# A block of extra matmul runs, copies and transfers behind the last norm of a two-layer encoder trunk

## The chip, the cores and the metric

The kernel runs as one program on 1 core of one Trainium2 chip. The metric is device time in microseconds (us) of that core for one execution. A profiled execution has a span, from the first to the last instruction that the profile shows, and its own device time, which is a little longer.

## The reference

The reference is a hybrid bidirectional encoder of `DEPTH = 2` layers over one sequence of 512 positions with 1024 channels, all in float32:

```python
for l in range(DEPTH):
    xn = rms_norm(x, ln1[l])
    z = xn @ w_in[l]                       # one combined projection
    y_a = ...                              # gated linear recurrence, forward and backward
    y_b = spatial_gating(...)              # 128x128 position mixing
    y_c = window_attention(...)            # banded grouped-query attention
    merged = (gates[:, :, 0] * (y_a @ w_br[l, 0])
              + gates[:, :, 1] * (y_b @ w_br[l, 1])
              + gates[:, :, 2] * (y_c @ w_br[l, 2]))
    x = x + merged @ w_out[l]
    hn = rms_norm(x, ln2[l])
    x = x + jnp.square(jax.nn.relu(hn @ w_up[l])) @ w_down[l]
return rms_norm(x, final_norm)
```

Only the last line and the end of the second layer's MLP stand next to the change.

## The kernel before

All work is written in one function, `trunk`, over a tile framework: tiles come from pools by a tag with a fixed number of buffers (`T("rb", ...)`, `T("jk", ...)`, `PT("m", ...)` for PSUM), and a scheduler decides when each instruction is put into its engine's queue. It works by priority (by default the order of the program text) among the instructions whose inputs are ready in its own timeline, and it places the semaphores. `tc.issue_after(ins)` adds an edge of issue order behind `ins`; by the framework's code, only instructions of the same engine as `ins` get it. Each engine's queue is then executed in order.

Every large matmul is made from split operands: a float32 value is cast on ScalarE to the type fp32r (`wh`, `xh`, `sh`), the rest is taken by subtraction on VectorE (`wl`, `xl`), and three matmuls make one product. Their moving operand is read in "pairs" order: `pairs(t)` reads column 0, column 256, column 1, column 257 and so on, with 512 columns in all. Plain float32 matmuls (attention, transposes) read contiguously. Weights come in chunks `ws[i]` of 128 x 1024 float32 (512 KB) by DMAs from the SP queue into `wr` or `wq` tiles; the `wq` tag has 10 buffers.

The end of the program is the last quarter (`qd == 3`) of the second layer's MLP. `down` runs `seven`, a scheme of seven block products per half, and as results leave PSUM, `done` adds up the squares of a row block and `finish` scales it and sends it out:

```python
def finish(ts):
    ...
    nc.gpsimd.tensor_tensor(rc, ss, mhalf_t[:, 0:n], ALU.pow)
    for i, t in enumerate(ts):
        nc.scalar.activation(xr[t][0], xr[t][0], AF.Copy, scale=rc[:, i:i + 1])
        nc.vector.scalar_tensor_tensor(xr[t][1], xr[t][1], rc[:, i:i + 1], fn_t[1], ALU.mult, ALU.mult)
        for fl in range(2):
            q = nc.scalar if (t, fl) == (1, 0) else nc.sync
            q.dma_start(out[:, t, fl * S:(fl + 1) * S], xr[t][fl])
```

It is called for row blocks 2 and 3 together, then for block 0, and last for block 1. After it the pools are closed and the program ends. The tile `z4` (128 x 2048, one buffer) holds the final norm's weights `fn_t` at that point, and `wq` holds the last chunks of the down projection.

Of the kernel before, what the change touches and what calls it, by code (L numbers as in the profile page):

```python
# [6 lines left out]
F32 = mybir.dt.float32  # L7
F32R = mybir.dt.float32r
U8 = mybir.dt.uint8
AF = mybir.ActivationFunctionType  # L10
ALU = mybir.AluOpType

P = 128
S = 512
# [5 lines left out]
CW = 1024  # L20
# [9 lines left out]
def ap_of(t, off, dims):  # L30
    return bass.AP(tensor=t.tensor, offset=t.offset + off, ap=[t.ap[0]] + dims)
# [11 lines left out]
def natural(t):  # L43
    return t.rearrange("p (a b) -> p a b", a=2)


def sorted_(pt):

    return ap_of(pt, 0, [[1, 2], [2, S // 2]])


def _chunk_keys():
# [26 lines left out]
def trunk(tc, x0v, xT, xt, ws, fnb, bsb, snk, wst, rope, cmask, amask, ident, out):  # L79
    nc = tc.nc  # L80
# [3 lines left out]
    def pool(**kw):  # L84
        p = tc.tile_pool(**kw)
        pools.append(p)
        return p.__enter__()

    cst = pool(name="cst", bufs=1)
    sb = pool(name="sb", bufs=1)  # L90
# [3 lines left out]
    dram = pool(name="dram", bufs=1, space=bass.MemoryType.DRAM)  # L94
# [11 lines left out]
    part = {}  # L106
# [4 lines left out]
    def nm(s):  # L111
        ctr[0] += 1
        return f"{s}_{ctr[0]}"

    def T(tag, name, dt=F32):
        where = part[HOME[tag]] if tag in HOME else sb
        return where.tile([P, S], dt, tag=tag, bufs=SLOTS[tag], name=nm(name))

    def begin(which):
        part[which] = pool(name=nm(which), bufs=1)  # L120
# [8 lines left out]
    def Z4(name):  # L129
        z4[:] = [sb.tile([P, 4, S], F32, tag="z4", bufs=1, name=nm(name)), 0]  # L130
        return z4[0]
# [8 lines left out]
    def SM(tag, w):  # L140
        return pad.tile([P, w], F32, tag="sm_" + tag, bufs=4 if tag == "lb" else NSM, name=nm(tag))
# [7 lines left out]
    def PT(tag, name):  # L149
        return ps.tile([P, S], F32, tag="p_" + tag, bufs=BANKS[tag], name=nm(name))  # L150
# [101 lines left out]
    def proj_part(xs, pt, w, ks):  # L252

        hi, lo = w
        for k in ks:
            c = slice(k * P, (k + 1) * P)
            i = mm3(pt, hi[:, c], lo[:, c], xs[k][0], xs[k][1], k == 0, k == KT - 1)
        return i

    def proj(xs, name, *key, bank="m"):  # L260

        return proj_w(xs, name, wload(*key), bank=bank)
# [139 lines left out]
    def two(pr, i):  # L402
        return tuple(x[:, i * HT:(i + 1) * HT] for x in pr)
# [359 lines left out]
    for i in range(2):  # L763
        c = slice(i * S, (i + 1) * S)
# [20 lines left out]
    for i in range(8):  # L785
        t = T("tv", "xt")
# [11 lines left out]
    for l in range(DEPTH):  # L798
        xs = n1.xs

        def evac(pt, tag, name):
            t = T(tag, name)
            with hp():
                nc.vector.tensor_tensor(natural(t), sorted_(pt), natural(n1.rb), ALU.mult)
            return t

        def a_ffb(h):
            z2 = Z2("z2") if h else None
            parts = [z2[:, d] if h else T("zt", "z2") for d in range(2)]
            for d in range(2):  # L810
                pt = proj(xs, f'f{h}', l, 'f', h, d)
                with hp():
                    nc.vector.tensor_tensor(natural(parts[d]), sorted_(pt), natural(n1.rb), ALU.mult)
            return a_gates(l, h, z2 if h else parts, lbs)
# [48 lines left out]
        bv = [None] * 4  # L863
# [68 lines left out]
        if l == 0:  # L932
            amask_t = cst.tile([P, 7 * P], U8, name="amask_t")
            for i in range(2):
                w = slice(i * 448, (i + 1) * 448)
# [15 lines left out]
        run = a_head(l, 0, *head_0, vt, oa)  # L951
# [14 lines left out]
        for g in range(4):  # L966
            pt = PT("s", "mx")
# [20 lines left out]
        def merge_b(d):  # L988
            z = evac(proj(xs, "gz", l, "gz", d), "l2", "gz")
            with hp():  # L990
                nc.scalar.activation(z, z, AF.Tanh, scale=0.5)
            if d % 2 == 0:
                wbr[0] = wload(l, "yb", d // 2)
            yp = proj_w(ys, "yB", wbr[0], (d % 2) * 4)
            m = T("g", "mg")
            with hp():
                nc.vector.scalar_tensor_tensor(natural(m), natural(z), 1.0, sorted_(yp), ALU.add, ALU.mult)
            nc.gpsimd.dma_start(mgd[:, d], m)
# [46 lines left out]
        pt = PT("c", "vT")  # L1045
# [101 lines left out]
        with later(30000):  # L1147
# [5 lines left out]
            for fl in range(2):  # L1153
                th = gates("ch", 0, fl)
                pts = proj_tok(ys, "yC", (l, "y", 2, fl), 0)
                for t in range(4):
                    if fl == 0:
                        kept.append(T("l", "mC"))
                    m = th[t] if fl else kept[t]
# [51 lines left out]
        xr = [[T("l", "xr"), T("l", "xr")] for _ in range(4)]  # L1211
# [19 lines left out]
        i = proj_part(n2.xs, *first[0], range(4))  # L1231
# [18 lines left out]
        last = l + 1 == DEPTH  # L1250
        Z4("u")
        n1 = norm_tok("ln1", l + 1, xr, True, 1.0 / math.sqrt(D) if last else 1.0)
        acc = [[T("tv", "acc"), T("tv", "acc")] for _ in range(4)]
        fn_t = []

        def finish(ts):

            n = len(ts)
            ss = SM("s4", 4)[:, 0:n]
            nc.vector.scalar_tensor_tensor(ss, ap_of(n1.ss, 2 * ts[0], [[2, n]]), EPS, ap_of(n1.ss, 2 * ts[0] + 1, [[2, n]]), ALU.add, ALU.add)  # L1260
            rc = SM("rs", 4)[:, 0:n]
            nc.gpsimd.tensor_tensor(rc, ss, mhalf_t[:, 0:n], ALU.pow)
            for i, t in enumerate(ts):
                nc.scalar.activation(xr[t][0], xr[t][0], AF.Copy, scale=rc[:, i:i + 1])
                nc.vector.scalar_tensor_tensor(xr[t][1], xr[t][1], rc[:, i:i + 1], fn_t[1], ALU.mult, ALU.mult)
                for fl in range(2):
                    q = nc.scalar if (t, fl) == (1, 0) else nc.sync
                    q.dma_start(out[:, t, fl * S:(fl + 1) * S], xr[t][fl])

        def done(t, fl):  # L1270

            n1.add(t, fl)
            if not last:
                nc.gpsimd.dma_start(xspill[:, t, fl * S:(fl + 1) * S], xr[t][fl])
            if last:
                if fl == 0:
                    nc.vector.tensor_tensor(xr[t][0], xr[t][0], fn_t[0], ALU.mult)
                if (t, fl) in ((0, 1), (1, 1)):
                    finish((t,))
                elif (t, fl) == (3, 0):  # L1280
                    finish((2, 3))
            elif t % 2:
                n1.turn(fl, (t - 1, t), "ssaa" if (t, fl) == (1, 1) else "ssss")

        for qd in range(4):
# [11 lines left out]
            for f in range(8):  # L1297
                if qd == 0 and f < 3:
                    pt = first[f][0]
                    proj_part(n2.xs, *first[f], range(4, KT))  # L1300
                else:
                    pt = proj(n2.xs, f'up{qd}', l, "up", qd, f, bank="c" if qd == 0 and f == 3 else "m")
# [21 lines left out]
        if not last:  # L1324
# [4 lines left out]
            end("mlp")  # L1329
            begin("G")  # L1330
        xsrc = xspill

    for p in reversed(pools):
        p.__exit__(None, None, None)
# [124 lines left out]
```

## Time and profile before

| | before |
|---|---|
| median of 2 runs | 1632.4 us (1631.79 to 1633.01) |
| profiled execution, its own time | 1631.72 us |
| span of the profiled execution | 1629.6 us |
| instructions | 21891 |
| PE busy | 1606.6 us (99% of the span) |
| DVE busy | 1288.0 us (79%) |
| ACT busy | 990.8 us (61%) |
| POOL busy | 117.2 us (7%) |

The engines are PE (TensorE matmul), PEld (its weight loads), DVE (VectorE), ACT (ScalarE), POOL (GpSimd) and SP (SyncE, which here only issues DMAs). In a timeline row the first number is the start in us from the span's start, the second the time that the merged piece takes, then engine, line, operation, output<-input, shape and count; what an engine waited for stands in brackets. Matmuls are pipelined, so the rate of a run of matmuls is read from start to start, not from one matmul's duration.

### The profile page before, as it was taken

Reading aid. Unit: us, or ns where it says so; the run is one execution under the profiler, and the core shown is the slowest. Engines: PE = TensorE matmul, PEld = TensorE weight load, DVE = VectorE, ACT = ScalarE, POOL = GpSimd, SP = SyncE. Lnnn points to the kernel's source line nnn. Section 1 sums busy time; section 2 is a strip of 40 time slices with the busy share of each in tenths; the row PEclk is TensorE's granted clock in tenths of the full one; section 3 lists DMA queues with packets and bytes.
Section 4 is the critical chain, followed back from the end, with each engine's and each line's share of the span. In section 5 each row is a group of like instructions: output and inputs, shape, how many; then the busy total and the mean of one; then the engine's idle time right before and its main releaser. Section 6 shows DMA issues by size and latency. Waiting matters only on the chain.

```text
span 1629.6 us, 21891 instructions
## 1 busy us (share of the span) xinstructions
PE 1606.6 (99%) x8034; PEld 1411.1 (87%) x8034; DVE 1288.0 (79%) x2015; ACT 990.8 (61%) x1695; POOL 117.2 (7%) x169
## 2 busy tenths in 40 slices
PE   9999999999999999999999999999999999999997
PEld 8888888998888888888888888888898888888886
DVE  7996998785666768697989969987856677686967
ACT  7576678775245664545766667688753365545464
POOL 1021000011200000000010210000103000000000
PEclk9999999999999999999999999999999999999999
DMA  8342221232555323233423422212226453332321
GB/s 334 121 149 97 83 89 53 78 104 98 197 197 197 113 104 104 104 104 104 143 93 124 172 96 78 91 59 85 84 98 223 177 194 104 103 108 100 125 69 52
DMA packets 58138, 195.83 MB, mean 120 GB/s; under 512 B 7504, under 2 KB 7888, under 8 KB 58032
## 3 DMA queue, kind: packets, MB, share of 16 engines
q1 hardware_dynamic: 47520, 160.23, 28.2%
q0 software_dynamic: 10368, 33.96, 5.9%
q8 instruction: 63, 1.03, 0.3%
q14 instruction: 43, 0.35, 0.1%
q10 hardware_dynamic: 144, 0.26, 0.0%
HBM read 175.54 MB, written 18.87 MB: 119 GB/s over the span
## 4 chain that ended last, share of the span: by engine, by line
PE 72%; DVE 12%; issue 6%; ACT 6%; DMA 2%; POOL 1%; SPq 0%; POOLq 0%; DVEq 0%; ACTq 0%
PE up L250 7%; PE up L248 7%; PE up L249 7%; PE dA L467 3%; PE dA L468 3%; PE dA L466 3%; DVE wl L243 2%; DVE ex L667 2%; PE wo L299 2%; PE wo L300 2%; PE dC L467 2%; PE wo L301 2%; PE dC L466 2%; PE at L625 2%; PE dC L468 2%
## 5 line engine op out<-in xcount | busy, mean ns | idle before, releaser
L242 ACT CAST wh<-wq 128x1024 fp32r<-128x1024 f32 x201 | 210.3, 1047 | 169.5 <-PE dA L467 42.7
L243 DVE TENSOR_TENSOR wl<-wq,wh 128x1024 fp32r<-128x1024 f32 x201 | 244.1, 1219 | 85.6 <-ACT wh L242 84.6
L243 DVE TENSOR_TENSOR wl<-wr,wh 128x1024 fp32r<-128x1024 f32 x166 | 203.3, 1225 | 129.7 <-ACT wh L242 124.0
L242 ACT CAST wh<-wr 128x1024 fp32r<-128x1024 f32 x166 | 173.3, 1045 | 211.4 <-PE up L249 55.4
L248 PE MATMUL up<-xh,wh 128*128 128x512 f32 x512 | 194.2, 379 | 0.0
L249 PE MATMUL up<-xl,wh 128*128 128x512 f32 x512 | 194.0, 379 | 0.0
L250 PE MATMUL up<-xh,wl 128*128 128x512 f32 x512 | 193.1, 379 | 0.0
L250 PEld LDWEIGHTS up<-xh,wl 128*128 128x128 f32 x512 | 96.8, 189 | 13.7
L248 PEld LDWEIGHTS up<-xh,wh 128*128 128x128 f32 x512 | 96.8, 189 | 13.7
L249 PEld LDWEIGHTS up<-xl,wh 128*128 128x128 f32 x512 | 96.8, 189 | 13.7
L466 PE MATMUL dA<-wh,sh 128*128 128x512 f32 x256 | 97.1, 379 | 0.0
L467 PE MATMUL dA<-wh,sh 128*128 128x512 f32 x256 | 97.0, 379 | 0.0
L468 PE MATMUL dA<-wl,sh 128*128 128x512 f32 x256 | 90.3, 379 | 0.0
L667 DVE TENSOR_TENSOR ex<-ex 128x512 f32<-128x512 f32 x112 | 80.4, 735 | 3.1 <-ACT key L647 3.0
L625 PE MATMUL at<-qt,kt 128*128 128x128 f32 x448 | 64.1, 276 | 1.7 <-ACT yh L307 0.6
L639 ACT ACTIVATE qt<-ex 128x512 f32<-128x512 f32 x56 | 37.6, 671 | 42.4 <-DVE ex L667 25.5
L625 PEld LDWEIGHTS at<-qt,kt 128*128 128x128 f32 x448 | 58.3, 192 | 4.6 <-ACT on L726 0.9
L307 ACT CAST sh<-sf 128x512 fp32r<-128x512 f32 x64 | 39.6, 618 | 25.2 <-DVE sf L430 18.1
L468 PEld LDWEIGHTS dA<-wl,sh 128*128 128x128 f32 x256 | 48.4, 189 | 6.8
L466 PEld LDWEIGHTS dA<-wh,sh 128*128 128x128 f32 x256 | 48.4, 189 | 6.8
L467 PEld LDWEIGHTS dA<-wh,sh 128*128 128x128 f32 x256 | 48.4, 189 | 6.8
L1079 ACT ACTIVATE sc<-sc,mx 128x256 f32<-128x256 f32 (+1 forms) x64 | 35.3, 553 | 25.3 <-DVE mx L1077 25.3
(414 smaller groups left out, 4303.3 us busy)
## 6 DMA issues: line engine op xcount, KB each, us to landing
wr<-in_ws_dram SPq DMA_DIRECT2D x166, 512.0 KB, 3.3
wq<-in_ws_dram SPq DMA_DIRECT2D x117, 512.0 KB, 4.4
thd<-zt POOLq DMA_DIRECT2D x32, 256.0 KB, 2.5
th<-thd POOLq DMA_DIRECT2D x32, 256.0 KB, 3.2
mgd<-mg POOLq DMA_DIRECT2D x16, 256.0 KB, 2.4
mB<-mgd POOLq DMA_DIRECT2D x16, 256.0 KB, 5.8
xt<-in_xt_dram SPq DMA_DIRECT2D x8, 256.0 KB, 7.6
mcd<-th POOLq DMA_DIRECT2D x8, 256.0 KB, 3.2
```

What stands on the lines that cost most here:

```text
L242: cast_i[0] = nc.scalar.copy(hi, raw)
L243: nc.vector.tensor_tensor(lo, raw, hi.bitcast(F32), ALU.subtract)
L248: nc.tensor.matmul(o, whi, xh, start=first, stop=False)
L249: nc.tensor.matmul(o, whi, xl, start=False, stop=False)
L250: return nc.tensor.matmul(o, wlo, xh, start=False, stop=last)
L307: nc.scalar.copy(hi, src)
L466: nc.tensor.matmul(o, xh[:, t], h, start=start and k == 0, stop=False, skip_group_check=True)
L467: nc.tensor.matmul(o, xl[:, t], h, start=False, stop=False, skip_group_check=True)
L468: return nc.tensor.matmul(o, xh[:, t], l_, start=False, stop=k == 3, skip_group_check=True)
L625: nc.tensor.matmul(pt[:, c], kk(st), qq[:, c], start=True, stop=True)
L639: nc.scalar.activation(qt.rearrange(shp, b=nb, h=2), e_q, AF.Exp)
L667: nc.vector.tensor_tensor(o_ap, o_ap, ap_of(ex, i_, [[istep, 2]] + z), ALU.add)
```

## The change

A new function `bench` is called once, after both layers, with `last_out[0]`, the first half of the row block that `finish` scaled last. It computes nothing that the output reads. The recording line in `finish` is the only change to what was there.

```diff
+def bench(tc, nc, sb, dram, ws, PT, T, Z4, part, nm, last):
+    V = nc.vector
+    wh = sb.tile([P, CW], F32R, tag="wh", bufs=3, name=nm("bwh"))
+    wl = sb.tile([P, CW], F32R, tag="wl", bufs=3, name=nm("bwl"))
+    f32 = T("rb", "bf")
+    V.tensor_copy(f32, last)
+    for t in (wh, wl):
+        nc.scalar.copy(t[:, 0:S], f32)
+        nc.scalar.copy(t[:, S:], f32)
+    prev = [None]
+    sink = T("jk", "bs")
+
+    def run(n, rhs, cols, w):
+        pt = PT("m", "bm")
+        o = pt[:, 0:cols]
+        ...
+        for i in range(n):
+            c = slice((i % 4) * P, (i % 4 + 1) * P)
+            with tc.issue_after(prev[0].ins) if prev[0] is not None else contextlib.nullcontext():
+                prev[0] = nc.tensor.matmul(o, w[:, c], rhs, start=i == 0, stop=i == n - 1)
+        V.tensor_copy(sink[:, 0:cols], pt[:, 0:cols])
+        return pt
+
+    def two(t, n, gap):
+        return ap_of(t, 0, [[1, n // 2], [gap, 2]])
+
+    run(48, wh[:, 0:256], 256, wl)
+    run(48, two(wh, 256, 128), 256, wl)
+    run(48, two(wh, 256, 256), 256, wl)
+    run(48, two(wh, 128, 64), 128, wl)
+    run(24, wh[:, 0:384], 384, wl)
+    run(24, two(wh, 384, 192), 384, wl)
+    run(24, f32[:, 0:128], 128, f32)
+    run(24, two(f32, 128, 64), 128, f32)
+    run(12, f32[:, 0:256], 256, f32)
+    run(12, two(f32, 256, 128), 256, f32)
+    a = run(4, wh[:, 0:S], S, wl)
+    b = PT("c", "bs")
+    c = PT("c", "bt")
+    d = PT("a", "bv")
+    for _ in range(3):
+        nc.scalar.copy(b, a)                                              # A1
+        nc.scalar.copy(c, b)                                              # A2
+        nc.scalar.copy(d, f32)                                            # A3
+        nc.scalar.copy(f32, c)                                            # A4
+        nc.scalar.copy(natural(f32), sorted_(c))                          # A5
+        V.tensor_tensor(sink, sink, c, ALU.add)                           # V1
+        V.tensor_tensor(natural(sink), natural(sink), sorted_(c), ALU.add)# V2
+        V.tensor_tensor(c, f32, b, ALU.add)                               # V3
+        V.scalar_tensor_tensor(sink, c, 0.0, f32, ALU.max, ALU.mult)      # V4
+        V.scalar_tensor_tensor(sink[:, 0:256], f32[:, 0:256], 0.0, f32[:, 256:], ALU.max, ALU.mult)  # V5
+        V.tensor_copy(sink, d)                                            # V6
+    big = Z4("big").rearrange("p a b -> p (a b)")
+    q = [big[:, i * CW:(i + 1) * CW] for i in range(2)] + [part["wq"].tile([P, CW], F32, tag="wq", bufs=10, name=nm("bq")) for _ in range(6)]
+    with tc.issue_after(prev[0].ins):
+        nc.sync.dma_start(q[0], ws[0])
+        nc.sync.dma_start(q[1], ws[1])
+    for i in range(4):
+        with tc.issue_after(prev[0].ins):
+            nc.sync.dma_start(q[2 + i], ws[i])
+    for i in range(4):
+        nc.gpsimd.dma_start(q[2 + i], ws[i + 2], accum_op=ALU.add)
+    for i in range(4):
+        with tc.issue_after(prev[0].ins):
+            nc.sync.dma_start(q[6 + i % 2], ws[i + 20])
+    for _ in range(2):
+        V.tensor_tensor(big, big, big, ALU.add)
+        V.tensor_tensor(big.rearrange("p (a b) -> p a b", a=4)[:, :, 0:256], big.rearrange("p (a b) -> p a b", a=4)[:, :, 256:], big.rearrange("p (a b) -> p a b", a=4)[:, :, 0:256], ALU.subtract)
+        nc.scalar.copy(big, big)
...
+        last_out = [None]                          # beside fn_t, in the loop over layers
...
+                last_out[0] = xr[ts[-1]][0]        # in finish, behind the two scalings
...
+    bench(tc, nc, sb, dram, ws, PT, T, Z4, part, nm, last_out[0])   # behind both layers
```

The marks A1 to A5 and V1 to V6 are added here as names for the steps of the loop.

More of the change, by code (lines that the diff above doesn't have):

```diff
@@ L49, in sorted_ @@
     return ap_of(pt, 0, [[1, 2], [2, S // 2]])
+def bench(tc, nc, sb, dram, ws, PT, T, Z4, part, nm, last):
[12 more added lines that the diff above has]
+        o = pt[:, 0:cols]
+        if len(rhs.ap) == 3:
+            o = o.rearrange("p (a b) -> p a b", a=rhs.ap[1][1])
+        for i in range(n):
[49 more added lines that the diff above has]
+        nc.scalar.copy(big, big)
```

## The prediction

> **What bounds the kernel now.** I read the page's first parts, then the timeline of the last 10 us, because everything the change adds waits for the last norm.
>
> ```profile
> span 1629.6 us, 21891 instructions
> ...
> PE 1606.6 (99%) x8034; PEld 1411.1 (87%) x8034; DVE 1288.0 (79%) x2015; ACT 990.8 (61%) x1695; POOL 117.2 (7%) x169
> ```
>
> PE is busy for 99% of the span; the rest is the tail, which the timeline of the last microseconds shows:
>
> ```profile
> 1621.08 0.38 PE L468 MATMUL dA<-wl,sh 128*128 128x512 f32 x1
> ...
> 1624.27 0.55 POOL L1262 TENSOR_TENSOR rs<-s,mhalf_t 128x1 f32<-128x1 f32 x1 [1.70 <-DVE s L1260]
> 1624.86 0.72 ACT L1264 ACTIVATE xr<-xr,rs 128x512 f32<-128x512 f32 x1 [0.92 <-POOL rs L1262]
> 1624.86 0.75 DVE L1265 SCALAR_TENSOR_TENSOR xr<-xr,rs,u 128x512 f32<-128x512 f32 x1 [0.73 <-POOL rs L1262]
> 1625.61 0.40 ACTq L1268 DMA_DIRECT2D out_dram<-xr  x1
> ```
>
> The last matmul starts at 1621.08. The last `finish` is that of row block 1; its ScalarE half ends at 1624.86 + 0.72 = 1625.58, and this is the tile handed to `bench`. From there to 1629.6 only output transfers land and the engines close. So PE, DVE, ACT and POOL are all empty after 1625.6: whatever hangs on that tile is added behind it, with nothing of the old kernel to hide under.
>
> **The start of the new chain.** V copies the tile to `f32`, ACT casts it four times, the first matmul needs the first three (`wh` left, `wh` right ahead of it in order, `wl` left).
>
> ```profile
> L307 ACT CAST sh<-sf 128x512 fp32r<-128x512 f32 x64 | 39.6, 618 | 25.2 <-DVE sf L430 18.1 <-DVE sf L433 7.1
> L938 DVE CAST amask_t<-am 128x448 uint8<-128x448 f32 x2 | 0.7, 376 | 0.0
> L308 DVE TENSOR_TENSOR sh<-sf,sh 128x512 fp32r<-128x512 f32 x64 | 43.8, 685 | 1.5 <-ACT sh L307 0.4
> ```
>
> The DVE copy of 512 columns isn't in the trace. Below stands the 448-column one-input cast, 0.38; above, the two-input 0.69. I take 0.41, the cast scaled up. The ACT casts cost 0.62 each, so PE starts at 1625.6 + 0.4 + 3 x 0.62 + 0.1 for the hand-overs = 1628.0. If the framework waits for all four casts it is 0.6 more.
>
> **The matmul runs.** Prices are start-to-start distances. The first four rows are split matmuls in pairs order, attention's plain float32 and its 128-column form; then come contiguous fp32r scores at 384 and 256 columns.
>
> ```profile
> 1190.27 0.38 PE L248 MATMUL ag<-xh,wh 128*128 128x512 f32 x1
> ...
> 1191.57 0.38 PE L248 MATMUL ag<-xh,wh 128*128 128x512 f32 x1
> ...
> 1192.21 1.05 PE L625 MATMUL at<-qt,kt 128*128 128x128 f32 x8
> 1193.11 0.60 PE L1106 MATMUL po<-pT,cvt 128*128 128x256 f32 x2
> ```
> ```profile
> 256.14 0.34 PE L1072 MATMUL sc<-k,q 128*128 128x384 f32 x1
> 256.32 0.34 PE L1073 MATMUL sc<-kl,q 128*128 128x384 f32 x1
> 256.49 0.27 PE L1101 MATMUL pT<-id_t,sc 128*128 128x128 f32 x1
> ```
> ```profile
> 213.67 0.28 PE L1073 MATMUL sc<-kl,q 128*128 128x256 f32 x1
> ...
> 214.03 0.38 PE L248 MATMUL yB<-yh,wh 128*128 128x512 f32 x1
> ```
> ```profile
> 239.85 1.03 PE L1106 MATMUL po<-pT,cvt 128*128 128x256 f32 x4
> 240.72 0.49 PE L1101 MATMUL pT<-id_t,sc 128*128 128x128 f32 x3
> ```
> ```profile
> L1106 PE MATMUL po<-pT,cvt 128*128 128x256 f32 x160 | 40.0, 380 | 0.0
> ```
>
> - Pairs order, fp32r: six matmuls of 512 columns in 1191.57 - 1190.27 = 1.30, 0.217 each. Halved, 0.109 for 256 columns; three quarters, 0.163 for 384.
> - Contiguous fp32r: 256 columns, three in 0.36, 0.120 each; 384 columns, two in 0.35, 0.175. Contiguous is a little dearer than its share of a pairs matmul.
> - Plain float32: `po` is called 80 times in the two layers (10 blocks per head pair, 4 pairs) and has 160 records, so one call is two passes. A pass takes 0.2175 at 256 columns (four in 0.87) and 0.1125 at 128 (eight in 0.90).
>
> Runs 1 to 11 in the order of the program:
> 1. 48 x 0.120 = 5.8
> 2. and 3. 48 x 0.109 = 5.2 each, 10.4
> 4. 128-column fp32r in pairs: no row has it. Below: a quarter of 0.217, 0.054, makes 2.6. Above: what plain float32 pays for 128 columns, two passes, 0.225, makes 10.8. I take 0.1125, one pass with a weight load of its own, the nearest row in size: 5.4. The ends stay in the range, 2.8 below and 5.4 above.
> 5. 24 x 0.175 = 4.2
> 6. 24 x 0.163 = 3.9
> 7. and 8. 24 x 0.225 = 5.4 each, 10.8
> 9. and 10. 12 x 0.435 = 5.2 each, 10.4
> 11. 4 x 0.22 = 0.9
>
> Sum 51.8. Between runs PE stands still for nothing: two "m" banks alternate, and a copy of 0.7 on DVE is over long before the bank's next turn.
>
> One sentence on what a page says of run 4: in the Trainium skill, "TensorE: Matmul & The Clock Gate", section "LDWEIGHTS (loading the stationary operand)", a weight load takes its columns divided by 1.2 GHz, by which I estimate 0.107 a matmul and 5.1 for the run; no row here shows a weight load as the bound.
>
> **The clock.** PE has been still since 1621.5 when the runs start.
>
> ```profile
> 1624.70:1629.60 4.90, 0.00 (x0) 0.00 (x0) 0.75 (x1) 0.72 (x1) 0.12 (x1) 0.50 0.47 176
> ```
> ```profile
> 1.05 4.64 PE L186 MATMUL warm<-warm 128*128 128x512 f32 x10 [1.05 <-DVE warm L183]
> 5.48 1.66 PE L248 MATMUL bu<-xh,wh 128*128 128x512 f32 x4
> 6.98 1.03 PE L249 MATMUL bu<-xl,wh 128*128 128x512 f32 x4
> ```
>
> In the view by stretches (behind the busy times of the five engines stands the granted clock) the clock is 0.50 from 1624.7 on. The start of the program shows the price: 14 matmuls take 6.98 - 1.05 = 5.93, where at 0.217 they would take 3.04. I add this 2.9 to run 1; the bounds are 0 and twice that.
>
> A page gives another size: the Trainium skill, "TensorE: Matmul & The Clock Gate", section "Part 1: The HAM clock gate (the 'warmup' mystery)", has the full clock back after about 3.4 us of sustained work, which at half speed would cost an estimated 1.7. The sum would be 1.2 lower by it; the start here shows 2.9.
>
> PE thus ends at 1628.0 + 51.8 + 2.9 + 0.2 for the last matmul's tail = 1682.9.
>
> **The copy loop.** It waits for run 11 (`a`), the last in PE's order.
>
> ```profile
> L645 ACT COPY at<-at 128x512 f32<-128x512 f32 x8 | 4.6, 580 | 1.4 <-PE at L625 1.3
> L1307 ACT ACTIVATE u<-up 128x512 f32<-128x512 f32 x64 | 37.8, 591 | 0.0
> L429 DVE TENSOR_TENSOR sf<-u 128x256 f32<-128x256 f32 x32 | 13.6, 424 | 0.4 <-ACT u L1308 0.4
> L1019 DVE TENSOR_TENSOR cq<-cq,sh 128x512 f32<-128x512 f32 x8 | 5.8, 731 | 0.0
> L516 DVE SCALAR_TENSOR_TENSOR xr<-dA,r,xr 128x512 f32<-128x512 f32 x16 | 11.5, 741 | 0.1
> ```
>
> An ACT copy out of PSUM is 0.58; the strided `sorted_` read of L1307 costs no more (0.59). Copies into PSUM have no row; I take 0.6. On DVE V3 0.69, V4 0.74, V5 0.42; V6 lies between 0.41 and 0.69, I take 0.69 for a PSUM source: 2.54.
> Round 1: A1, A2, A4, A5 in a chain, 2.4 (A3 needs only `f32` and can go ahead during the runs); V1 and V2 (0.69 + 0.73) start behind A2 and end at 2.6. Then V3 to V6, each on the result or the tile of the one before, 2.54. Rounds 2 and 3: A1 needs V3 and A2 needs V4, both hidden beside V4 to V6, but A3 overwrites `d`, which V6 reads, and A4 overwrites `f32`, which A3 reads: 3 x 0.6 = 1.8, with V1 and V2 beside it, then 2.54. A hand-over takes 0.04 (L1262 ends at 1624.82, its readers start at 1624.86); with 0.4 for those of the loop: 2.6 + 3 x 2.54 + 2 x 1.8 + 0.4 = 14.2. Loop ends at 1697.1.
>
> **What I cost at nothing.** The two passes over `big` need only `q[0]` and `q[1]`.
>
> ```profile
> L606 ACT ACTIVATE ex<-ex 128x2048 f32<-128x2048 f32 x4 | 7.7, 1916 | 0.0
> L243 DVE TENSOR_TENSOR wl<-wq,wh 128x1024 fp32r<-128x1024 f32 x201 | 244.1, 1219 | 85.6 <-ACT wh L242 84.6
> wq<-in_ws_dram SPq DMA_DIRECT2D x117, 512.0 KB, 4.4
> mC<-mcd POOLq DMA_DIRECT2D x8, 256.0 KB, 9.4
> ```
>
> A pass is 2.3 (DVE, 2048 columns, twice the 1219 ns row less one overhead) + 1.2 + 1.9 = 5.4, two of them 10.8 plus hand-overs, 11. The loads overwrite `z4`, free at 1625.6, and land 4.4 later, about 1630; DVE and ACT are empty until 1683 but for short result copies, so the scheduler can place all of it under the runs. Without that cover it is 11 at the end.
> SP: the order edges name a PE instruction, and the framework applies them only to PE's, so the ten loads are not held; six can start as `wq` buffers fall free from about 1600 on, the two to `big` wait in SP's queue for 1625.6 with output transfers near them, which matter no longer.
> POOL: the four accumulating transfers have no row. Below stands the plain SP load of that size, 4.4, so 18 for four; above, the slowest POOL row (9.4 for 256 KB), doubled for size and one after the other, 75. From 1610 even that ends at 1685, before the loop does. So nothing.
>
> **The sum.** After the last work the engines close in about 1.0 (the outputs have long landed). Span 1698.1, that is 68.5 more; 1631.72 + 68.5 = 1700.2 in the profiled execution's terms; the median of the runs is 0.7 above it: **1701**.
>
> **Rivals.**
> - *`big` comes last*: the scheduler's order keeps the text's order on DVE. For it: the text puts it last. Against it: the scheduler works by what is ready, and DVE and ACT have nothing else for 50 us. 1701 + 11 = 1712.
> - *POOL holds something up*: an accumulating transfer queued ahead of L1262 makes the norm wait for its load, or four of them outlast the loop. The point is a load landing after 1619, or over 22 us a transfer. Price 5 to 40: 1706 to 1741.
> - *Pairs with small distances read slower*: the rows show distance 256 only. Doubled fp32r pairs runs (2, 3, 4, 6) are 19.7: 1721. The Trainium skill, "SBUF — State Buffer", section "Door 1: The DMA port swizzle", charges each access that leaves a 16-byte line; the pairs rows at 0.217 against 0.120 for half as many contiguous columns do not agree.
> - *Not slower*: nothing reads `bench`'s results; if the build drops unread work, place: all eleven runs, price -68: 1633. It decides once over 36 of the 68 is gone. Against it: the ten `warm` matmuls above, whose result is never read, ran.
> - *Everything at its low end* (run 4 at 2.6, no slow clock, short V6): 1694 and below.
>
> **How the numbers follow.** Forecast (1693 to 1709) 0.68; `big` last 0.10; POOL 0.10; pairs 0.04; dropped 0.03; low end below 1693 0.05. The range 1692 to 1716 holds the forecast, `big` last and half of POOL, over 0.8. Two per cent, about what a measurement of this kernel can tell, is 33 us: slower 0.97, within 0.03, faster 0.
>
> **What would show it.** PE's first new matmul near 1628 at clock 0.50 for some 5 us; runs at the distances above, run 4 anywhere from 0.054 to 0.225; the `big` instructions inside the runs' stretch; L1262 still near 1624; the loop about 14 us. Wrong would make it: distances over 0.13 at 256 columns, accumulations landing after 1695, copies into PSUM far from 0.6.

## The result and the profile after

The changed kernel takes 1706.87 us (median of 1705.36 and 1708.38) against 1632.4 before: a ratio of 1.0456, 95% interval 1.0411 to 1.0501. The profiled execution took 1705.36 with a span of 1703.4, so the span grew by 73.8. The forecast was 1701 with a growth of 68.5.

The first parts of the page of the changed kernel:

```profile
span 1703.4 us, 22771 instructions
...
PE 1662.2 (98%) x8422; PEld 1463.8 (86%) x8422; DVE 1312.4 (77%) x2049; ACT 1005.4 (59%) x1716; POOL 120.7 (7%) x173
```

PE has 388 matmul records and 55.6 us more. The rest of the 73.8 lies where PE does nothing: ahead of run 1 and behind run 11.

The timeline of VectorE in the changed kernel; L1339 is the last norm's scaling, L58 the copy to `f32`, L74 the copy of a run's result, which starts some 0.2 us behind the run's last matmul (the first two are held up by the work on `big`):

```profile
1623.98 0.75 DVE L1339 SCALAR_TENSOR_TENSOR xr<-xr,rs,u 128x512 f32<-128x512 f32 x1 [0.73 <-POOL rs L1336]
1624.73 0.43 DVE L58 COPY bf<-xr 128x512 f32<-128x512 f32 x1
1632.24 2.29 DVE L120 TENSOR_TENSOR big<-big 128x2048 f32<-128x2048 f32 x1 [7.08 <-DMA big<-in_ws_dram]
...
1645.25 0.42 DVE L74 COPY bs<-bm 128x256 f32<-128x256 f32 x1 [3.59 <-PE bm L73]
1650.56 0.29 DVE L74 COPY bs<-bm 128x128 f32<-128x128 f32 x1 [4.88 <-PE bm L73]
1654.78 0.56 DVE L74 COPY bs<-bm 128x384 f32<-128x384 f32 x1 [3.93 <-PE bm L73]
1658.68 0.56 DVE L74 COPY bs<-bm 128x384 f32<-128x384 f32 x1 [3.34 <-PE bm L73]
1664.04 0.29 DVE L74 COPY bs<-bm 128x128 f32<-128x128 f32 x1 [4.80 <-PE bm L73]
1670.59 0.29 DVE L74 COPY bs<-bm 128x128 f32<-128x128 f32 x1 [6.26 <-PE bm L73]
1675.77 0.42 DVE L74 COPY bs<-bm 128x256 f32<-128x256 f32 x1 [4.89 <-PE bm L73]
1682.32 0.42 DVE L74 COPY bs<-bm 128x256 f32<-128x256 f32 x1 [6.13 <-PE bm L73]
1683.24 0.69 DVE L74 COPY bs<-bm 128x512 f32<-128x512 f32 x1 [0.49 <-PE bm L73]
1686.41 0.69 DVE L100 TENSOR_TENSOR bs<-bs,bt 128x512 f32<-128x512 f32 x1 [2.47 <-ACT bf L99]
...
1692.34 0.69 DVE L100 TENSOR_TENSOR bs<-bs,bt 128x512 f32<-128x512 f32 x1 [1.89 <-ACT bf L99]
...
1701.64 0.69 DVE L105 COPY bs<-bv 128x512 f32<-128x512 f32 x1
```

From the row of run 3 (1645.25) on, each row less the one before is the length of a run: run 4 takes 5.31, runs 5 and 6 4.22 and 3.90, run 7 5.36, run 8 6.55, run 9 5.18, run 10 6.55, run 11 0.92. Runs 7 and 8 have the same matmuls and differ only in the order of the moving columns; so do 9 and 10. V1 (L100) waits for A5 (L99), in the first round (1686.41) as in the second (1692.34); the third, at 1698.28, has the same wait of 1.89.

PE in the changed kernel's timeline, and ScalarE around the last matmul:

```profile
1626.96 31.68 PE L73 MATMUL bm<-bwh,bwl 128*128 128x256 f32 x240 [6.39 <-ACT bwl L60]
```
```profile
1683.97 0.57 ACT L95 COPY bs<-bm 128x512 f32<-128x512 f32 x1 [40.71 <-DVE bs L74]
...
1685.79 0.59 ACT L99 COPY bf<-bt 128x512 f32<-128x512 f32 x1
```

The first matmul starts at 1626.96. A1 (L95) starts at 1683.97, released not by PE but by VectorE's copy of run 11 (L74, 1683.24 + 0.69). The loop then lasts until 1701.64 + 0.69 = 1702.33: 18.4.

Account of the profiled span, forecast against trace:

| term | forecast | trace |
|---|---|---|
| last norm's scaling ends | 1625.6 | 1624.7 |
| copy and casts to the first matmul | 2.4 | 2.3 |
| run 1 with the slow clock | 8.7 | 7.4 |
| runs 2 and 3 | 10.4 | 10.7 |
| run 4 | 5.4 | 5.3 |
| runs 5 to 7 | 13.5 | 13.5 |
| run 8 | 5.4 | 6.55 |
| run 9 | 5.2 | 5.2 |
| run 10 | 5.2 | 6.55 |
| run 11 and the last tail | 1.1 | 1.1 |
| from there to A1 | 0 | 0.7 |
| copy loop | 14.2 | 18.4 |
| closing | 1.0 | 1.1 |
| span | 1698.1 | 1703.4 |

Run 1 is the time from 1626.96 to run 3's copy, less 0.2 and less runs 2 and 3 at 0.1117 a matmul (96 of them, 10.7).

### The profile page after: what moved, and what is told of

Same layout as the page of the kernel before. It is cut to its first block, busy times and chain, and to the rows that moved or that the text cites. A ratio compares the mean times of both kernels' runs of the same rounds, so it can differ in the third digit from the quotient of the medians.

```text
span 1703.4 us, 22771 instructions
## 1 busy us (share of the span) xinstructions
PE 1662.2 (98%) x8422; PEld 1463.8 (86%) x8422; DVE 1312.4 (77%) x2049; ACT 1005.4 (59%) x1716; POOL 120.7 (7%) x173
## 4 chain that ended last, share of the span: by engine, by line
PE 72%; DVE 13%; ACT 6%; issue 5%; DMA 2%; POOL 1%; SPq 0%; POOLq 0%; DVEq 0%; ACTq 0%
PE up L323 6%; PE up L321 6%; PE up L322 6%; PE bm L73 3%; PE dA L541 3%; PE dA L540 3%; PE dA L539 3%; DVE wl L316 2%; DVE ex L740 2%; PE wo L372 2%; PE wo L373 2%; PE dC L540 2%; PE wo L374 2%; PE dC L539 2%; PE dC L541 1%
## 5 line engine op out<-in xcount | busy, mean ns | idle before, releaser
L321 PE MATMUL gz<-xh,wh 128*128 128x512 f32 x128 | 49.5, 387 | 0.9 <-DVE gz L877 0.9
```

What stands on the lines that cost most here:

```text
L321: nc.tensor.matmul(o, whi, xh, start=first, stop=False)
```

## The experiments

The unaltered kernel (e1_again) ran beside e2, e3 and e4 as a measure. e5 to e8 ran later on another chip, e5 to e7 once each, so there the traces decide. In the edits, comments are added here and `...` stands for lines left out.

**e1_again.** No edit.

> The changed kernel once more, unaltered, as the measure for the runs beside it. Its two executions so far lie 3.0 us apart (1705.36 and 1708.38), those of the kernel before 1.2. Theory: the slow-clock phase of the first matmul run has a length that differs from execution to execution (3.5 us in the profile of the changed kernel, 5.9 at the start of the profile before), so the matmul runs take 56 to 58 us and the whole 1705 to 1709. Rival: the spread lies in the old part of the program, which ended 0.9 us earlier in the profile after than in that before; then the eleven runs take 56.3 again whatever the total.

Measured: 1707.3 us median of 1705.99 to 1708.21, ratio 1.0454 (1.0438 to 1.0469). The view by stretches shows its PE and clock (behind the busy times of the five engines):

```profile
1627.60:1631.00 3.40, 3.40 (x16) 3.40 (x17) 0.00 (x0) 0.95 (x2) 0.00 (x0) 0.50 0.92 308
1631.00:1633.80 2.80, 2.80 (x15) 2.80 (x15) 1.58 (x1) 0.00 (x0) 0.00 (x0) 0.50 0.08 26
1633.80:1636.10 2.30, 2.30 (x21) 2.30 (x21) 1.94 (x2) 0.30 (x1) 0.00 (x0) 1.00 0.00 0
```

The same view of the first changed execution:

```profile
1626.90:1630.40 3.50, 3.44 (x16) 3.44 (x17) 0.00 (x0) 1.01 (x3) 0.00 (x0) 0.50 0.97 342
1630.40:1634.30 3.90, 3.90 (x34) 3.90 (x34) 2.06 (x1) 0.00 (x0) 0.00 (x0) 0.99 0.08 29
```

The slow phase lasted 3.5 us there and 6.2 here; run 1 took 7.4 and 8.6. That part of the theory holds. The rival holds a part too: the spans of these two profiles differ by 1.8 us, 1.2 of it in run 1 and 0.65 ahead of it (the norm's scaling ends at 1624.73 and at 1625.38). In e2, whose edit lies far behind the norm, it ends at 1626.89, and the kernel before spread over 2.5 us itself (1631.76 to 1634.22 in seven runs), as much as this one (2.2).

**e2_v_reads_b.**

```diff
-        V.tensor_tensor(sink, sink, c, ALU.add)
-        V.tensor_tensor(natural(sink), natural(sink), sorted_(c), ALU.add)
+        V.tensor_tensor(sink, sink, b, ALU.add)
+        V.tensor_tensor(natural(sink), natural(sink), sorted_(b), ALU.add)
```

> In the copy loop the two VectorE sums V1 and V2 read the PSUM tile b in place of c; the values are the same. Theory: V1 waits for A5 only because both read the tile c, whose accesses from two engines the framework puts one after the other; with b, V1 and V2 run beside A4 and A5 (round 1) and A3 to A5 (rounds 2 and 3), and the loop falls from 18.4 us by 1.2 + 2 x 1.45 = 4.1 to about 14.3, the figure of the prediction. Rival: VectorE and ScalarE can't read PSUM at the same time at full rate, or V1 waits for something else; then V1 still starts at A5's end or its row grows from 0.69 toward 1.2, and the loop stays above 17.

Measured: 1703.55, ratio 1.0429 (1.0411 to 1.0446), 3.75 less than beside it. Timelines of VectorE and ScalarE:

```profile
1688.16 0.69 DVE L100 TENSOR_TENSOR bs<-bs,bs 128x512 f32<-128x512 f32 x1 [1.24 <-ACT bt L96]
...
1700.39 0.69 DVE L105 COPY bs<-bv 128x512 f32<-128x512 f32 x1
```
```profile
1686.96 0.57 ACT L95 COPY bs<-bm 128x512 f32<-128x512 f32 x1 [42.31 <-DVE bs L74]
...
1688.16 0.59 ACT L98 COPY bf<-bt 128x512 f32<-128x512 f32 x1
```

V1 now waits for A2 and starts at the same 1688.16 as A4, with its row still at 0.69 us: both engines read PSUM, each its own tile, and neither is slowed. The loop lasts 1686.96 to 1701.08, 14.1 in place of 18.4. What held V1 was that A4 and A5 read the same tile.

**e3_no_side.** The block from `big = ...` to the end of `bench` is left out.

> Left out: the loads to big and wq, the four accumulating transfers and the two passes over big; runs and loop stay. Theory of the prediction: all of this is hidden under the runs, so the time stays within 1 us of the unaltered kernel. Rival: transfers and passes slow the chain (the norm's POOL step, the result copies, the casts); then 2 us or more are gained.

Measured: 1707.82, ratio 1.0455 (1.044 to 1.0471), beside 1.0454 for the unaltered kernel. All transfers and both passes over `big` cost nothing that these runs can tell.

**e6_side_alone.** The other way round: only that block is kept, without its order edges, as there are no runs to name.

> Left out: the runs, the copies into f32, wh, wl and the whole loop; the loads, the four accumulating transfers and the two passes over big stay, with nothing to hide under. Theory: the passes start when the loads to big land (about 7 us after the last norm) and take 11 us, so the span is 1629.6 + 14 to 16 = about 1644 to 1646, and the accumulating transfers have landed long before. Rival: the accumulating transfers end last; then a wait on them stands at the end of the chain and the span is longer than 1648.

Measured: one execution of 1647.48, span 1645.5. VectorE in its timeline and the DMA view of its last 60 us:

```profile
1626.15 0.75 DVE L1288 SCALAR_TENSOR_TENSOR xr<-xr,rs,u 128x512 f32<-128x512 f32 x1 [0.73 <-POOL rs L1285]
...
1633.54 2.29 DVE L69 TENSOR_TENSOR big<-big 128x2048 f32<-128x2048 f32 x1 [6.64 <-DMA big<-in_ws_dram]
```
```profile
bq<-in_ws_dram POOLq DMA_DIRECT2D x4, 512.0 KB, 9.2
```

Uncovered, the block adds 15.9 to the span of 1629.6: 6.6 of waiting for the loads, 11.0 for the passes (1633.54 to 1644.54) and 1.0 of closing in place of the 4.0 behind the norm before, and the norm itself ended 1.3 later. Under the runs the same work is free. An accumulating transfer of 512 KB lands in 9.2 us (the median of four), half the upper bound of the prediction, and e3 shows no cost of it.

**e4_clock_kept.**

```diff
+    last_mm = [None]
...
+                            last_mm[0] = mm
...
+    wz = sb.tile([P, CW], F32R, tag="wl", bufs=WB, name=nm("wz"))[:, 0:S]
+    nc.vector.memset(wz.bitcast(F32), 0.0)
+    zp = PT("s", "keep")
+    with tc.issue_after(last_mm[0].ins):           # behind the last matmul of the down projection
+        for _ in range(24):
+            nc.tensor.matmul(by_two(zp), wz[:, 0:P], pairs(wz), start=True, stop=True)
     bench(...)
```

> Added: 24 fp32r matmuls of 512 columns on zeros behind the last matmul of the down projection, while the last norm runs (24 x 0.216 = 5.2 us of a gap of 5.9). Theory: run 1 is slow (0.213 a matmul for its first 16) because PE stood still from 1621 to 1627 and its clock was at 0.50; kept busy, the clock stays at 1.00, run 1 takes 48 x 0.118 = 5.7 in place of 7.3, and the whole is 1.7 us shorter. Rival: the first matmuls are slow for another reason (fresh operands, instruction fetch), or zeros don't count as work; then run 1 stays above 7 us.

Measured: 1704.63, ratio 1.044 (1.0424 to 1.0456), 2.7 less than beside it, with intervals that overlap. The stretches of its trace decide:

```profile
1622.50:1628.40 5.90, 5.35 (x25) 4.35 (x23) 2.75 (x5) 4.13 (x9) 1.10 (x2) 1.00 0.95 347
1628.40:1634.30 5.90, 5.85 (x49) 5.85 (x50) 1.31 (x1) 1.00 (x2) 0.00 (x0) 1.00 0.56 191
```

With the clock at 1.00 all 48 matmuls of run 1 fit into the 5.9 us in which e1_again does about 29 (16 in 3.4, then 15 in 2.8). Run 1 takes 5.85. So the slow clock cost 1.5 in the first profiled execution and 2.7 in e1_again. The timelines of two others bear it out: the 240 fp32r matmuls of runs 1 to 6 last 30.16 here, and 32.52 in e2 and 32.33 in e3, so 2.4 and 2.2 more; e3 has no transfers beside run 1 that could have slowed it.

**e5_forms.** Runs 1 to 10 replaced:

```diff
+    H, L = wh.bitcast(F32), wl.bitcast(F32)
+    run(48, two(wh, 256, 256), 256, wl)
+    run(48, two(wh, 64, 32), 64, wl)
+    run(48, wh[:, 0:128], 128, wl)
+    run(24, two(f32, 128, 64), 128, f32)
+    run(24, two(f32, 128, 128), 128, f32)
+    run(24, two(f32, 128, 256), 128, f32)
+    run(24, two(H, 128, 512), 128, L)
+    run(24, ap_of(f32, 0, [[2, 128]]), 128, f32)          # step 2
+    run(24, ap_of(f32, 0, [[1, 32], [64, 4]]), 128, f32)  # fours
+    run(24, ap_of(f32, 0, [[128, 2], [1, 64]]), 128, f32) # two blocks
+    run(48, ap_of(wh, 0, [[2, 256]]), 256, wl)            # fp32r, step 2
+    run(24, wh[:, 0:512], 512, wl)
+    run(24, two(wh, 512, 256), 512, wl)
+    run(24, f32[:, 0:64], 64, f32)
```

> Runs 1 to 10 are replaced by fourteen runs of other forms; everything else stays. Distances from start to start decide, not the total. Question one, the floor under 128-column fp32r (0.1105 in run 4). Theory: the weight load that goes with each matmul sets it, so 64 columns in pairs take 0.11 too, contiguous 128 fp32r 0.11, and a pass of plain float32 at 64 columns also 0.11. Rival: below 256 columns fp32r takes two array cycles a column, so 64 columns take 0.055 to 0.06. Question two, plain float32 in pairs order (0.1366 a pass at 128 columns against 0.1116 contiguous). Theory: leaving the run of neighbouring columns at every element costs it, whatever the distance: 0.137 at distances 64, 128, 256 and with another weight tile at 512, 0.137 in fours of distance 64, and 0.112 for two contiguous blocks. Rival A: the distance 64 or 128 matters; then 256 and 512 give 0.112. Rival B: weights and moving columns from the same tile collide; then the run with the other weight tile gives 0.112. Contiguous fp32r at 512 columns 0.231 against 0.216 in pairs; every second column (step 2, 256 columns fp32r) 0.112 if a jump helps fp32r, 0.118 or more if not.

Measured: one execution, 1752.08. The VectorE copies behind the runs of distance 64 (first row) to the last:

```profile
1660.98 0.29 DVE L74 COPY bs<-bm 128x128 f32<-128x128 f32 x1 [7.58 <-PE bm L73]
1667.54 0.29 DVE L74 COPY bs<-bm 128x128 f32<-128x128 f32 x1 [6.27 <-PE bm L73]
1674.10 0.29 DVE L74 COPY bs<-bm 128x128 f32<-128x128 f32 x1 [6.27 <-PE bm L73]
1680.66 0.29 DVE L74 COPY bs<-bm 128x128 f32<-128x128 f32 x1 [6.27 <-PE bm L73]
1686.10 0.29 DVE L74 COPY bs<-bm 128x128 f32<-128x128 f32 x1 [5.15 <-PE bm L73]
1696.76 0.29 DVE L74 COPY bs<-bm 128x128 f32<-128x128 f32 x1 [10.37 <-PE bm L73]
1702.12 0.29 DVE L74 COPY bs<-bm 128x128 f32<-128x128 f32 x1 [5.07 <-PE bm L73]
1713.01 0.42 DVE L74 COPY bs<-bm 128x256 f32<-128x256 f32 x1 [10.59 <-PE bm L73]
1718.47 0.69 DVE L74 COPY bs<-bm 128x512 f32<-128x512 f32 x1 [5.04 <-PE bm L73]
1723.65 0.69 DVE L74 COPY bs<-bm 128x512 f32<-128x512 f32 x1 [4.49 <-PE bm L73]
1728.95 0.22 DVE L74 COPY bs<-bm 128x64 f32<-128x64 f32 x1 [4.61 <-PE bm L73]
```

Differences over the number of passes (48 for plain float32, else the number of matmuls): pairs at distance 128, 256 and, with another weight tile, 512: 6.56 / 48 = 0.137 each. So neither the distance among these nor a shared tile is the cause; rivals A and B fall. Step 2 takes 0.113, fours 0.222, two blocks 0.112. fp32r with step 2: 0.227 for 256 columns, twice the pairs; contiguous 512 columns 0.2275 and pairs 0.216. Plain float32 at 64 columns: 0.110 a pass, as at 128. Halving the columns saves nothing: there is a floor of 0.11 under each pass. The weight load, 128x128 in every run, would fit as its cause, but every run also has one such load per pass, so a fixed price of each matmul fits as well; no run has other weights, and that part of the theory stays open.

The 64-column fp32r run lost the full clock on its way, with no pause on PE, and the contiguous 128-column run behind it never had it:

```profile
1635.70:1639.30 3.60, 3.60 (x36) 3.60 (x34) 1.97 (x3) 1.90 (x1) 0.00 (x0) 1.00 0.00 0
...
1642.50:1652.80 10.30, 10.30 (x50) 10.30 (x50) 0.23 (x1) 1.19 (x1) 0.00 (x0) 0.50 0.00 0
```

The 64-column run starts at about 1635.8 and the clock falls at about 1639.4, 3.6 us later. All 48 contiguous matmuls of 128 columns then run at 0.50, 0.214 each, for 10.3 us without a pause, and do not bring the clock back; it returns at about 1656.4, in the plain float32 run behind them. e7 has both forms again.

**e7_forms2.** Fifteen more forms in the same place, of which these matter:

```diff
...
+    run(48, wh[:, 0:128], 128, wl)
...
+    run(24, two(H, 128, 60), 128, L)
+    run(24, two(H, 128, 66), 128, L)
+    run(24, two(H, 128, 2), 128, L)
+    run(24, ap_of(f32, 0, [[1, 64], [0, 2]]), 128, f32)   # each column twice
+    run(24, ap_of(f32, 0, [[4, 128]]), 128, f32)          # step 4
+    run(24, ap_of(H, 0, [[8, 128]]), 128, L)              # step 8
+    run(48, ap_of(wh, 0, [[1, 64], [64, 4]]), 256, wl)    # fp32r, fours
+    run(24, two(wh, 512, 2), 512, wl)
+    run(48, two(wh, 512, 256), 512, wl)
+    run(300, two(wh, 64, 32), 64, wl)
+    run(24, two(wh, 512, 256), 512, wl)
```

> Runs 1 to 10 are replaced by fifteen runs of other forms; everything else stays. Distances from start to start decide. Question one, plain float32 in pairs (0.1366 a pass at distances 64, 128, 256 and 512, against 0.112 contiguous or in two blocks, 0.113 with step 2, 0.222 in fours). Theory: a column costs more when it doesn't lie beside the one before in memory, so distances 60 and 66 give 0.137 too, while distance 0 (each column twice) and 2 stay at 0.112; step 4 and step 8 give 0.137 or more. Rival: the two-level pattern itself costs it, so distances 0 and 2 give 0.137 and step 4 gives 0.112. Question two, fp32r: in fours 0.22 or more for 256 columns if it is like step 2 (0.228), 0.112 if only steps hurt; pairs at distance 2 (512 columns) 0.216 or, if like step 2, 0.44. Contiguous 128-column fp32r at the full clock 0.111, the floor of the weight load; if fp32r contiguous pays more below 256 columns, 0.12 or more. Question three: in the run of forms the granted clock fell to 0.50 behind 48 matmuls of 64 columns, without any pause on PE. Theory: at 64 columns the array works too small a part of the time to hold the clock; 300 of them then run at 0.111 for at most 10 us and at 0.213 after that, and the 512-column run behind starts at 0.43. Rival: that fall was a single event; then all 300 take 0.111, 33 us in all.

Measured: one execution, 1817.07. The copies behind distance 256 (first row), 60, 66, 2, 0, step 4, step 8, fp32r fours and fp32r distance 2:

```profile
1660.50 0.29 DVE L74 COPY bs<-bm 128x128 f32<-128x128 f32 x1 [6.27 <-PE bm L73]
1667.06 0.29 DVE L74 COPY bs<-bm 128x128 f32<-128x128 f32 x1 [6.27 <-PE bm L73]
1672.66 0.29 DVE L74 COPY bs<-bm 128x128 f32<-128x128 f32 x1 [5.31 <-PE bm L73]
1678.02 0.29 DVE L74 COPY bs<-bm 128x128 f32<-128x128 f32 x1 [5.07 <-PE bm L73]
1683.38 0.29 DVE L74 COPY bs<-bm 128x128 f32<-128x128 f32 x1 [5.07 <-PE bm L73]
1694.26 0.29 DVE L74 COPY bs<-bm 128x128 f32<-128x128 f32 x1 [10.59 <-PE bm L73]
1705.45 0.29 DVE L74 COPY bs<-bm 128x128 f32<-128x128 f32 x1 [10.90 <-PE bm L73]
1712.05 0.42 DVE L74 COPY bs<-bm 128x256 f32<-128x256 f32 x1 [6.30 <-PE bm L73]
1717.24 0.69 DVE L74 COPY bs<-bm 128x512 f32<-128x512 f32 x1 [4.77 <-PE bm L73]
```

A plain float32 pass of 128 columns: distance 60 0.137, 66 0.117, 2 and 0 0.112, step 4 0.227, step 8 0.233. The two-level pattern as such is free, so the rival falls; but the theory missed 66 and gave no size for step 4 and step 8, and step 2, free in e5, does not fit it. What fits is that the cost follows where the columns lie in memory. The distances from 60 on that are multiples of 4 columns (16 bytes) cost 0.137 and 66, which is none, 0.117; why is open, one value being too few. fp32r: fours 6.60 / 48 = 0.138, which is neither of the two values that had been named, and distance 2 at 512 columns 0.216, the full rate.

The clock, by stretches: contiguous fp32r at 128 columns, then the 300 matmuls of 64 columns:

```profile
1641.80:1647.10 5.30, 5.30 (x49) 5.27 (x49) 1.09 (x2) 1.91 (x1) 0.00 (x0) 1.00 0.00 0
1727.40:1733.00 5.60, 5.60 (x52) 5.59 (x51) 0.69 (x1) 0.00 (x0) 0.00 (x0) 1.00 0.00 0
1733.00:1786.00 53.00, 53.00 (x251) 53.00 (x250) 0.00 (x0) 0.00 (x0) 0.00 (x0) 0.50 0.00 1
```

128 columns contiguous: 0.11 at full clock, the floor again. With 64 columns the clock fell to 0.50 after 5.6 us of the run and stayed there for all the rest (251 in 53 us, 0.211 each, so the floor doubles with the halved clock). What the theory forecast came, and the fall in e5 was no single event. That the array works too small a part of the time is its reason, and no run tests that by itself.

**e8_account.** The edits of e2 and e4, and

```diff
-    run(24, two(f32, 128, 64), 128, f32)
+    run(24, f32[:, 0:128], 128, f32)
...
-    run(12, two(f32, 256, 128), 256, f32)
+    run(12, f32[:, 0:256], 256, f32)
...
-        V.tensor_copy(sink[:, 0:cols], pt[:, 0:cols])
+        if n > 4:
+            V.tensor_copy(sink[:, 0:cols], pt[:, 0:cols])
+        else:
+            V.tensor_copy(sink, f32)
```

> All corrections to the prediction at once: V1 and V2 read b; runs 8 and 10 are contiguous like 7 and 9; 24 matmuls on zeros keep the clock at 1.00 through the norm; the copy of run 11's result on VectorE is replaced by a copy from f32, so A1 has no other reader of its PSUM tile ahead of it. Theory: the terms add, against the unaltered kernel (1707.3): 4.3 for the loop, 2.6 for the two runs, 1.5 to 2.7 for the clock, 0.7 for A1's wait, 9.1 to 10.3 in all, so 1697 to 1698. Rival: some of them lie beside each other and not behind each other; then 1700 or more.

Measured: 1698.0, ratio 1.0393 (1.0376 to 1.0411). That is 9.3 under e1_again, with the kernel before at 1633.27 beside it and 1633.04 beside e1_again. The terms add, as far as these runs can tell (9.1 to 10.3 had been expected). By the rows of the result copies, runs 8 and 10, now contiguous, take 5.36 and 5.18 like 7 and 9, where they took 6.55 each in pairs: the order alone made the difference. A1 is now released by PE:

```profile
1681.42 0.57 ACT L98 COPY bs<-bm 128x512 f32<-128x512 f32 x1 [35.01 <-PE bm L73]
```

## Why the prediction was right, and where its sum was off

The direction, the place and most of the sum held. The block is a tail with nothing to hide under; the side work is hidden under the runs (e3, e6); the halved and scaled distances for fp32r held to 3%; run 4 took the middle value, one pass on a floor of 0.11 (0.1105 against 0.1125), not the two passes of plain float32. The row for it was of another type and chosen for its size; that both types share that floor was seen only in e5, so the closeness is in part luck. The estimate from the Trainium skill, "TensorE: Matmul & The Clock Gate", section "LDWEIGHTS (loading the stationary operand)", 5.1 for that run, lies near the 5.31 of the trace. The 64-column runs (0.11) show a floor there that the trace of before could not, but not that the weight load sets it.

The total was 5.3 us of span too low. Three terms were 7.4 too low together and two others 2.2 too high:

- *The copy loop, +4.2.* The step that failed is that V1 and V2 "start behind A2" and that rounds 2 and 3 run "with V1 and V2 beside it". V1 waited for A5 in every round, since A4, A5 and V1 read one PSUM tile and the program orders such accesses across engines, reads too. e2 removed it with another tile and gave 14.1 where the prediction had 14.2.
- *A1, +0.7.* The same thing, overlooked at "It waits for run 11": VectorE's copy of run 11 reads the same tile and went first. e8 took it away.
- *Plain float32 in pairs, +2.5.* Runs 8 and 10 were priced as 7 and 9, from contiguous rows. Their passes take 0.137 and 0.273 where contiguous ones take 0.112 and 0.216, and e8 has them at the contiguous time. Small, but the wrong way: pairs are the cheaper order for fp32r and the dearer for plain float32.
- *The slow clock, -1.3, and an earlier start, -0.9.* The 2.9 came from the start of the program, where the rows run at half rate but the granted clock reads 1.00 in the view (the trace has no clock record before 6.76), so that the clock as the cause was argued there; e4 shows it for run 1. Measured, the slow clock cost 1.5 here and 2.7 in e1_again. The estimate of 1.7 from the Trainium skill, "TensorE: Matmul & The Clock Gate", section "Part 1: The HAM clock gate (the 'warmup' mystery)", fits the first execution (3.5 us slow) and not the second (6.2 us). The norm's end moved between the profiled executions (1624.73, 1625.38 and 1626.89 in the first, e1_again and e2), and the work ahead of it is the same in these three; that is the spread of the old part. That these two terms offset 2.2 of the 7.4 is luck: with the norm's end and the slow clock of e2 they would have offset nothing.

Of the rivals, `big` last, POOL and the dropped block did not come. The rival on pairs was half there: it named runs 2, 3, 4 and 6, where nothing happened (0.1117 at distance 128 as at 256), and set the plain float32 runs aside.

## What to carry to other kernels

When two engines read one PSUM tile, count their reads one behind the other, and give one of them another tile if it stands on the path. Price a run of matmuls from a row with the same type and the same column order, and don't scale it down below the 0.11 us a matmul that 128 and 64 columns both took at the full clock. Behind a pause of PE allow for a slow phase whose length changes from execution to execution, and don't judge 1 to 2 us by single runs.

## What the runs showed of the hardware that had not been expected

- A clock that falls without any pause: back-to-back 64-column fp32r matmuls, 0.111 us apart, lost the full clock 3.6 us (e5) and 5.6 us (e7) into their run and went on at 0.211. 128-column ones kept it over the 5.3 us of one run (e7), which may be too short to tell, and in e5 did not win it back in 10.3 us; 256-column ones won it back within 3.5 to 6.2 us.
- In the traces' clock records the stretches at 0.50 in the tail last 6.83 us in the first execution, e2 and e3, 10.24 in e1_again, 17.07 from the 64-column run of e5 on and 58.03 from that of e7 on: 2, 3, 5 and 17 times 3.41. Run 1 meets what is left of such a stretch when it starts, which fits a slow phase that differs from execution to execution. No run tests this.
- The order of the moving columns has a price that depends on the type: at 256 columns fp32r takes 0.112 in pairs, 0.12 contiguous, 0.138 in fours, 0.227 with step 2; a plain float32 pass of 128 columns takes 0.112 contiguous, 0.113 with step 2, 0.137 in pairs, 0.222 in fours, 0.227 with step 4.
- A PSUM-to-PSUM copy on ScalarE takes 0.57 us for 128x512, no more than one to SBUF (0.59).
